# HGRN2 level products: one run and one PSUM bank per head half

## The chip, the cores and the metric

The kernel runs on one core of a Trainium2 chip. The metric is the device time of one execution in microseconds. Three runs of the kernel before took 2713.78, 2715.27 and 2718.02 us; the median is 2715.27 us. The profile comes from one further execution, which took 2714.48 us and whose span, from its first to its last instruction, is 2712.6 us.

## The reference

One layer of a hybrid decoder over 2048 prompt tokens and 32 sample tokens of width 1024: RMSNorm, an input projection whose columns feed four mixers (S5, HGRN2, RWKV-7, pooling), an output projection with a residual, RMSNorm, a squared-ReLU MLP with a residual, and a last RMSNorm. The change lies in the HGRN2 mixer, a gated linear recurrence:

```python
def step(S, inp):
    qb, kb, vb, gb = inp
    b = jnp.cumsum(gb, axis=2)
    diff = jnp.where(causal, b[:, :, :, None, :] - b[:, :, None, :, :], -jnp.inf)
    att = jnp.einsum('bhtk,bhsk,bhtsk->bhts', qb, kb, jnp.exp(diff))
    o = jnp.einsum('bhts,bhsv->bhtv', att, vb) + jnp.einsum('bhtk,bhkv->bhtv', qb * jnp.exp(b), S)
    ...
```

The kernel works on chunks of 64 tokens. `att` needs the decay between every two tokens of a chunk. It is built in levels: for a distance h of 32, 16, 8, 4, 2 and 1, the later half of each group of 2h tokens meets its earlier half, with both decays taken against the token in the middle. Every level is a matrix product of its own, of which a mask keeps the entries that belong to the level; the diagonal is a seventh product.

## The kernel before

The tokens go through in six blocks of 256 or 384 (`BLK`). Per block the main work is three dense stages, the input projection (`inproj`), the output projection (`outproj`) and the MLP (`mlp`). Their matmuls are at L157 to L159, three for each pair of 128x128 weights and tokens, since weights and activations are split into a high and a low part (L128 on ScalarE, L129 on VectorE). There are 13248 of them.

Beside the main work run the mixers of the next block as side work. `mixers` alternates between two lanes: `lane1` is RWKV-7, and `lane2` is pooling, then HGRN2 (`hgrn_pair`, once for each 128 tokens, so 16 times in all), then S5. Lanes are Python generators: each `yield` ends a step, and `drive` takes `RATIO` = 2 side steps for each step of the main work. In the first stage (blocks 0 and 1) `weave` and a `drive` with other ratios do the same. The steps set the order in which instructions are emitted; a scheduler of the framework then places them on the engines' queues by its own estimate of when each is ready. So the order on an engine is not simply that of the code, and it is fixed before the run.

In `hgrn_pair`, a pair is two chunks (`cp`) of 64 tokens, four heads as two tiles (`j`) of two halves (`hp`, 64 partitions each). Per pair the level part is this:

- 8 diagonal products (64x64 by 64x64) and 48 level products (64x64 by 64x32), all at L1272. They are float32, and the trace holds two records for each: 16 and 96 per pair.
- They go in two passes: first the diagonal and levels 0 and 1, then levels 2 to 5 (`for l0, l1 in ((-1, 2), (2, 6))`). Each pass takes two new PSUM buffers (`pas`, one for each head half) with 256 of their 512 columns in use. The lane has two such buffers in all (`PX`), so the second pass needs both back from the first.
- VectorE takes the results out after each pass: 2 multiplications with the diagonal mask (L1280) and 24 `copy_predicated` (L1287) per pair.
- Inside the first pass there is a `yield` after level 0 and inside the second one after level 3 (`YH`), then one after each pass's products and one after each pass's evacuation: six steps.

TensorE works with tiles: a 64x64 product uses a quarter of the array. In the profile the tile stands as 64\*64, 64\*128, 128\*64 or 128\*128 (rows and columns in use); the main matmuls are 128\*128.

Of the kernel before, what the change touches and what calls it, by code (L numbers as in the profile page):

```python
# [11 lines left out]
ALU = mybir.AluOpType  # L12
# [567 lines left out]
PX = (2, 2)  # L580
S0PM = True
PLATE = ()
YH, YS, YR = (0, 3), True, True


class Carve:
# [20 lines left out]
class Mix(Main):  # L607
# [580 lines left out]
    def hgrn_pair(self, b, c0, pool):  # L1188
        nc = self.nc
        tt, ts, stt = nc.vector.tensor_tensor, nc.vector.tensor_scalar, nc.vector.scalar_tensor_tensor  # L1190
        act, mm = nc.scalar.activation, nc.tensor.matmul
# [5 lines left out]
        q, f, v, gt = P[:, 2:4, W], P[:, 4:6, W], P[:, 6:8, W], P[:, 8:10, W]  # L1197
# [10 lines left out]
        k = T("E")  # L1208
# [9 lines left out]
        QK = T("QK", (128, 6, 256))  # L1218
# [19 lines left out]
        LV = (32, 16, 8, 4, 2, 1)  # L1238
        for li, h in enumerate(LV):
            nb = 256 // (2 * h)  # L1240
# [9 lines left out]
            O = QK[:, li, :].rearrange("p (j n s) -> p j n s", j=2, s=2 * h)[:, :, :, h:]  # L1250
            tt(out=O, in0=O, in1=q.rearrange("p j (n s) -> p j n s", s=2 * h)[:, :, :, h:], op=ALU.mult)

        for l0, l1 in ((-1, 2), (2, 6)):
            pas = [self.px() for _ in range(2)]
            sec = {}
            for l in range(l0, l1):
                o0 = 0 if l < 0 else 64 * (l - l0) + (64 if l0 < 0 else 0)
                w = 64 if l < 0 else 32
                for hp in range(2):
                    hs = slice(64 * hp, 64 * hp + 64)  # L1260
                    d = pas[hp][:, o0:o0 + 2 * w].rearrange("p (j n) -> p j n", j=2)
                    sec[l, hp] = d
                    for j in range(2):
                        for cp in range(2):
                            o = 128 * j + 64 * cp
                            if l < 0:
                                a, c = k[hs, j, 64 * cp:64 * cp + 64], q[hs, j, 64 * cp:64 * cp + 64]
                            else:
                                h = LV[l]
                                a = QK[hs, l, o:o + 64]  # L1270
                                c = a.rearrange("p (n s) -> p n s", s=2 * h)[:, :, h:]
                            mm(d[64 * cp:64 * cp + 64, j, :], a, c, start=True, stop=True)  # L1272
                if l in YH:
                    yield
            yield
            for l in range(l0, l1):
                for hp in range(2):
                    o, d = v[:, :, 64 * hp:64 * hp + 64], sec[l, hp]
                    if l < 0:
                        tt(out=o, in0=d, in1=self.C("i64")[:, None, :].to_broadcast([128, 2, 64]), op=ALU.mult)  # L1280
                        continue
                    h = LV[l]
                    nb = 32 // h
                    cut = lambda x: x.rearrange("p (n s) -> p n s", s=2 * h)[:, :, h:]
                    m = self.C("lv%d" % h).bitcast(mybir.dt.int32).rearrange("p (n s) -> p n s", s=h)
                    for j in range(2):
                        nc.vector.copy_predicated(cut(o[:, j, :]), m, d[:, j, :].rearrange("p (n s) -> p n s", s=h))  # L1287
            yield
        S = [self.S[:, (self.Si + i) % 3] for i in range(3)]
        self.Si = (self.Si + 2) % 3  # L1290
        pu = self.px()[:, :256].rearrange("p (c j n) -> p c j n", c=2, j=2)
# [8 lines left out]
        for j, cp, hp, o in jch:  # L1300
            w = slice(64 * cp, 64 * cp + 64)
            mm(po[o, j, w], VB[:, cp, 2 * j + hp, :], v[:, j, o], start=j == cp == 0, stop=False, skip_group_check=True)
        for j, cp, hp, o in jch:
            w = slice(64 * cp, 64 * cp + 64)
# [732 lines left out]
```

## Time and profile before

| | |
|---|---|
| median of three runs | 2715.27 us |
| the profiled execution | 2714.48 us |
| its span | 2712.6 us |
| TensorE busy (PE) | 2629.4 us, 97% |
| VectorE busy (DVE) | 1955.7 us, 72% |
| ScalarE busy (ACT) | 1438.6 us, 53% |
| mean granted TensorE clock | 0.982 of 2.4 GHz |

A matmul's record lasts longer than the array needs for it, since successive matmuls overlap; a row that says 0.34 us is followed by the next after about 0.175 us. So durations of TensorE's records are not added up here: what a stretch of matmuls takes is read from the start of one row to the start of a later one.

### The profile page before, as it was taken

The page shows a single profiled execution, that of the slowest core. Times are in us where ns is not written, and L with a number is a line of the kernel's source. Part 1 is how long each engine was busy: PE and PEld are TensorE (multiplying, and loading weights), DVE is VectorE, ACT ScalarE, POOL GpSimd, SP SyncE. Part 2 cuts the span into 40 slices and gives each one's busy share as a digit, 9 for nine tenths or more (in the row PEclk, how much of TensorE's full clock was granted, in tenths as well). Part 3 has the DMA queues.
Part 4 walks back from the last instruction along what each step waited for, and adds up shares of the span by engine and source line. Part 5 has one row for each costly group of instructions (what it writes and reads, how often), then busy time and mean ns, then how long its engine had stood idle before and what let it go on. Part 6 is the DMA issues. An engine that isn't in the chain of part 4 may idle for free.

```text
span 2712.6 us, 52883 instructions
## 1 busy us (share of the span) xinstructions
PE 2629.4 (97%) x20466; PEld 2492.0 (92%) x20466; DVE 1955.7 (72%) x4324; ACT 1438.6 (53%) x2377; POOL 357.5 (13%) x864
## 2 busy tenths in 40 slices
PE   8799899899999999999999999999999999999998
PEld 8688799889999999999999999999999989899997
DVE  7886888874877777487777748777775786557666
ACT  6544766544656545375654536565454754445443
POOL 7631201100111100001110010111001100000000
PEclk9799999999999999999999999999999999999999
DMA  6543344564333255532335553223555334435553
GB/s 208 142 126 98 124 148 134 156 190 147 115 96 98 96 166 165 166 119 88 99 101 174 167 160 113 94 91 107 173 177 159 100 103 122 133 115 169 167 168 127
DMA packets 221068, 366.28 MB, mean 135 GB/s; under 512 B 105520, under 2 KB 140912, under 8 KB 220816
## 3 DMA queue, kind: packets, MB, share of 16 engines
q1 hardware_dynamic: 220816, 362.90, 43.1%
q8 instruction: 161, 2.64, 0.4%
q14 instruction: 91, 0.75, 0.1%
HBM read 343.26 MB, written 17.99 MB: 133 GB/s over the span
## 4 chain that ended last, share of the span: by engine, by line
PE 74%; DVE 11%; DMA 5%; ACT 4%; POOL 3%; issue 2%; SPq 1%; DVEq 0%; ACTq 0%; POOLq 0%
PE mm L157 21%; PE mm L158 21%; PE mm L159 21%; DVE wlo L129 3%; DMA raw<-w 2%; PE x L1272 1%; ACT whi L128 1%; POOL XD L887 1%; POOL tm L885 1%; DMA xs<-xT 1%; PE x L687 1%; PE x L1828 1%; PE x L1827 1%; DMA mt<-dB 1%; PE x L951 1%
## 5 line engine op out<-in xcount | busy, mean ns | idle before, releaser
L128 ACT CAST whi<-raw 128x1024 fp32r<-128x1024 f32 x552 | 577.5, 1046 | 773.0 <-PE mm L158 528.0
L157 PE MATMUL mm<-AB,whi 128*128 128x384 f32 (+2 forms) x2880 | 950.4, 331 | 14.2 <-ACT whi L128 5.2
L159 PE MATMUL mm<-AB,wlo 128*128 128x384 f32 (+2 forms) x2880 | 936.2, 325 | 4.2 <-DVE wlo L129 3.8
L158 PE MATMUL mm<-AB,whi 128*128 128x384 f32 (+2 forms) x2880 | 935.2, 325 | 1.0 <-DVE AB L199 0.8
L129 DVE TENSOR_TENSOR wlo<-raw,whi 128x1024 fp32r<-128x1024 f32 x552 | 678.4, 1230 | 274.2 <-ACT whi L128 271.6
L157 PEld LDWEIGHTS mm<-AB,whi 128*128 128x128 f32 x2880 | 545.9, 190 | 27.3 <-ACT whi L128 6.3
L159 PEld LDWEIGHTS mm<-AB,wlo 128*128 128x128 f32 x2880 | 547.1, 190 | 9.3 <-DVE wlo L129 6.3
L158 PEld LDWEIGHTS mm<-AB,whi 128*128 128x128 f32 x2880 | 547.6, 190 | 6.7 <-DVE AB L199 1.4
L157 PE MATMUL mm<-act,whi 128*128 128x384 f32 (+2 forms) x1536 | 497.7, 329 | 4.6 <-ACT whi L128 2.5
L158 PE MATMUL mm<-act,whi 128*128 128x384 f32 (+2 forms) x1536 | 493.9, 323 | 0.5 <-DVE act L329 0.3
L159 PE MATMUL mm<-act,wlo 128*128 128x384 f32 (+2 forms) x1536 | 492.2, 322 | 0.0
L157 PEld LDWEIGHTS mm<-act,whi 128*128 128x128 f32 x1536 | 289.6, 190 | 12.9 <-DVE h L338 2.8
L158 PEld LDWEIGHTS mm<-act,whi 128*128 128x128 f32 x1536 | 291.2, 190 | 5.5 <-issue 2.3
L159 PEld LDWEIGHTS mm<-act,wlo 128*128 128x128 f32 x1536 | 290.6, 190 | 1.6 <-issue 0.2
L338 DVE TENSOR_TENSOR h<-h,mm 128x384 f32<-128x384 f32 (+2 forms) x384 | 192.5, 510 | 96.4 <-PE mm L159 95.6
L885 POOL TENSOR_TENSOR tm<-sq,XD 32x15 f32<-32x15 f32 (+7 forms) x240 | 90.7, 378 | 563.0 <-DMA sq<-XC 545.6
L329 DVE TENSOR_TENSOR act<-q,act 128x384 fp32r<-128x384 f32 (+2 forms) x192 | 98.9, 516 | 6.2 <-ACT q L326 1.7
L324 ACT ACTIVATE act<-r 128x384 fp32r<-128x384 f32 (+2 forms) x192 | 94.2, 490 | 13.3 <-DVE r L323 11.0
L887 POOL TENSOR_TENSOR XD<-XD,tm 32x15 f32<-32x15 f32 (+7 forms) x240 | 85.4, 356 | 18.5
L880 POOL MEMSET XD<- 32x512 f32 x16 | 8.3, 516 | 578.2 <-PE x L969 346.1
L192 DVE TENSOR_TENSOR acc<-acc,sq 128x384 f32<-128x384 f32 (+2 forms) x126 | 64.8, 514 | 15.7 <-ACT sq L191 13.3
L328 DVE TENSOR_TENSOR q<-r 128x384 f32<-128x384 f32 x128 | 71.1, 555 | 0.6 <-ACT r L321 0.5
(584 smaller groups left out, 3110.4 us busy)
## 6 DMA issues: line engine op xcount, KB each, us to landing
raw<-w SPq DMA_DIRECT2D x552, 512.0 KB
xs<-xT SPq DMA_DIRECT2D x96, 192.0 KB
yT<-xo SPq DMA_DIRECT2D x32, 192.0 KB
mt<-dB SPq DMA_DIRECT2D x20, 256.0 KB
mt<-dT SPq DMA_DIRECT2D x20, 256.0 KB
mt<-dC SPq DMA_DIRECT2D x20, 256.0 KB
xs<-xT SPq DMA_DIRECT2D x24, 144.0 KB
rt<-dRot SPq DMA_DIRECT2D x16, 98.0 KB
```

What stands on the lines that cost most here:

```text
L128: nc.scalar.copy(hi, raw)
L129: (nc.gpsimd if GW(i) else nc.vector).tensor_tensor(out=lo, in0=raw, in1=hi, op=ALU.subtract)
L157: nc.tensor.matmul(ps[:, :n], a, xh, start=k == ks[0], stop=False)
L158: nc.tensor.matmul(ps[:, :n], a, xl, start=False, stop=False)
L159: nc.tensor.matmul(ps[:, :n], c, xh, start=False, stop=k == ks[-1])
L192: nc.vector.tensor_tensor(out=acc[:, :n], in0=acc[:, :n], in1=q[:, :n], op=ALU.add)
L324: nc.scalar.activation(out=self.act[:, s, 0, :n], in_=r[:, :n], func=AF.Square)
L328: nc.vector.tensor_tensor(out=q[:, :n], in0=r[:, :n], in1=r[:, :n], op=ALU.mult)
L329: nc.vector.tensor_tensor(out=self.act[:, s, 1, :n], in0=q[:, :n], in1=self.act[:, s, 0, :n], op=ALU.subtract)
L338: nc.vector.tensor_tensor(out=self.h[:, d, :n], in0=self.h[:, d, :n], in1=ps[:, :n], op=ALU.add)
L885: g.tensor_tensor(out=w, in0=U[:, 0:t, t:t + 1].to_broadcast([32, t, m]), in1=XT[:, t:t + 1, t:16].to_broadcast([32, t, m]), op=ALU.mult)
L887: g.tensor_tensor(out=XT[:, 0:t, t:16], in0=XT[:, 0:t, t:16], in1=w, op=ALU.add)
```

## The change

The two passes become one. All seven products of a head half go to one PSUM buffer, the diagonal in columns 0 to 127 and level l in columns 128 + 64 l to 191 + 64 l: 512 columns, a full bank. The 56 products of a pair are emitted without a step between them. Then comes a `yield`, the evacuation of the diagonal and levels 0 and 1, a `yield`, the evacuation of levels 2 to 5, and a `yield`: three steps. Number, shape and operands of the products and of the evacuations stay, and so does their order in the code (`HO` puts the head half outermost, as the loops did).

```diff
-YH, YS, YR = (0, 3), True, True
+YS, YR = True, True
+HO = [(j, cp, hp) for hp in range(2) for j in range(2) for cp in range(2)]
...
-        for l0, l1 in ((-1, 2), (2, 6)):
-            pas = [self.px() for _ in range(2)]
-            sec = {}
-            for l in range(l0, l1):
-                o0 = 0 if l < 0 else 64 * (l - l0) + (64 if l0 < 0 else 0)
...
-                if l in YH:
-                    yield
-            yield
-            for l in range(l0, l1):
...
-            yield
+        pas = [self.px() for _ in range(2)]
+        sec = {}
+        for l in range(-1, 6):
+            w, o0 = (64, 0) if l < 0 else (32, 128 + 64 * l)
+            for hp in range(2):
+                sec[l, hp] = pas[hp][:, o0:o0 + 2 * w].rearrange("p (j n) -> p j n", j=2)
+            for j, cp, hp in HO:
...
+                mm(sec[l, hp][64 * cp:64 * cp + 64, j, :], a, c, start=True, stop=True)
+        yield
+        for l in range(-1, 6):
...
+            if l == 1:
+                yield
+        yield
```

In the changed kernel the products are at L1267 and the evacuations at L1273 and L1279. How the scheduler places them shows on TensorE in the second pair of block 3. Before, the pair's 56 products stand there in nine rows between the main matmuls (L157 to L159) and the products of the other lane (L687 sums over a head, L907, L908 and L913 transposes, L926 a 64x64 product); the first of them:

```order
L159 MATMUL mm<-AB_78,wlo 128x384
L1272 MATMUL x<-P_7462,E 64x64 x8
L1272 MATMUL x<-QK 64x32
L687 MATMUL x<-hi,bonesr 128x256
L687 MATMUL x<-lo,bonesr 128x256
L1272 MATMUL x<-QK 64x32 x2
L907 MATMUL x<-cst,Z 128x128
L908 MATMUL x<-cst,P_8323 128x128
L907 MATMUL x<-cst,Z 128x128
L908 MATMUL x<-cst,P_8323 128x128
L1272 MATMUL x<-QK 64x32 x5
L157 MATMUL mm<-act,whi 128x384
```

and most of the second pass of the same pair:

```order
L159 MATMUL mm<-act,wlo 128x384
L1272 MATMUL x<-QK 64x32 x4
L687 MATMUL x<-hi,bonesr 128x256
L799 MATMUL x<-tha,wl 128x128 x2
L687 MATMUL x<-lo,bonesr 128x256
L802 MATMUL x<-kx,wl 128x128 x2
L1272 MATMUL x<-QK 64x32 x12
L157 MATMUL mm<-act,whi 128x384
```

Of the changed kernel, the same pair (L988 is a product of the RWKV lane with 128\*64 tiles):

```order
L159 MATMUL mm<-AB_78,wlo 128x384
L1267 MATMUL x<-P_7569,E 64x64 x8
L1267 MATMUL x<-QK 64x32 x4
L988 MATMUL x<-sv,M_8879 64x64 x4
L1267 MATMUL x<-QK 64x32 x44
L157 MATMUL mm<-AB_78,whi 128x384
```

All 56 stand between two main matmuls now, with one piece of the other lane among them.

## Rows read from the trace of the kernel before

**Rows 1.** The page: the span, and busy time, share and instructions by engine.
```profile
span 2712.6 us, 52883 instructions
PE 2629.4 (97%) x20466; PEld 2492.0 (92%) x20466; DVE 1955.7 (72%) x4324; ACT 1438.6 (53%) x2377; POOL 357.5 (13%) x864
```

**Rows 2.** Windows: length, busy us by engine, granted clock, DMA share, GB/s.
```profile
85.00:135.00 50.00, 40.83 (x325) 35.85 (x324) 48.23 (x103) 28.57 (x51) 29.39 (x50) 0.80 0.58 155
...
0.00:135.00 135.00, 108.86 (x808) 100.03 (x809) 106.23 (x230) 77.13 (x133) 92.93 (x241) 0.86 0.59 176
135.00:365.00 230.00, 213.33 (x1943) 196.46 (x1942) 174.96 (x463) 128.82 (x229) 54.59 (x121) 0.95 0.41 122
365.00:640.00 275.00, 261.81 (x2462) 246.90 (x2463) 214.74 (x503) 157.71 (x263) 27.23 (x74) 0.98 0.49 152
640.00:1110.00 470.00, 468.78 (x3464) 446.14 (x3463) 337.81 (x734) 250.15 (x402) 47.68 (x115) 1.00 0.41 129
1110.00:1580.00 470.00, 469.50 (x3468) 446.78 (x3468) 337.37 (x734) 250.28 (x402) 48.00 (x115) 1.00 0.41 129
...
2050.00:2440.00 390.00, 381.64 (x2931) 355.17 (x2930) 267.06 (x639) 196.93 (x352) 38.43 (x81) 0.99 0.40 121
2440.00:2713.00 273.00, 256.19 (x1873) 254.32 (x1872) 179.57 (x286) 127.09 (x190) 0.00 (x0) 0.98 0.48 157
```

**Rows 3.** TensorE's longest waits: who for whom, us in total, times, longest.
```profile
PE x L1272 <- ACT E L1209: 8.5, 1, 8.5
PE mm L157 <- ACT whi L128: 7.7, 5, 2.8
```

**Rows 4.** Groups by shape, L1272: busy us, mean ns, idle before them.
```profile
L1272 PE MATMUL x<-QK 64*64 64x32 f32 x1536 | 52.1, 223 | 0.3 <-DVE P L1287 0.3
L1272 PE MATMUL x<-P,E 64*64 64x64 f32 x256 | 13.3, 232 | 11.1 <-ACT E L1209 8.5 <-ACT VB L1234 2.6
```

**Rows 5.** Timeline of TensorE from 755.6: start us, length us, instruction.
```profile
755.64 0.34 PE L158 MATMUL mm<-act,whi 128*128 128x384 f32 x1
755.82 0.33 PE L159 MATMUL mm<-act,wlo 128*128 128x384 f32 x1
756.08 0.45 PE L1272 MATMUL x<-QK 64*64 64x32 f32 x16
756.46 0.44 PE L157 MATMUL mm<-AB,whi 128*128 128x384 f32 x1
```

**Rows 6.** The same from 765.9.
```profile
765.89 0.34 PE L159 MATMUL mm<-AB,wlo 128*128 128x384 f32 x1
766.16 0.69 PE L1272 MATMUL x<-QK 64*64 64x32 f32 x32
766.78 0.45 PE L157 MATMUL mm<-AB,whi 128*128 128x384 f32 x1
```

**Rows 7.** The same from 875.3.
```profile
875.34 0.34 PE L159 MATMUL mm<-act,wlo 128*128 128x384 f32 x1
875.61 0.68 PE L957 MATMUL x<-XD,M 64*64 64x64 f32 x16
876.22 0.45 PE L157 MATMUL mm<-act,whi 128*128 128x384 f32 x1
```

**Rows 8.** The same from 920.1.
```profile
920.13 0.34 PE L159 MATMUL mm<-act,wlo 128*128 128x384 f32 x1
920.39 0.47 PE L926 MATMUL x<-Z 64*64 64x64 f32 x16
920.68 0.67 PE L1272 MATMUL x<-QK 64*64 64x32 f32 x32
921.27 0.44 PE L157 MATMUL mm<-act,whi 128*128 128x384 f32 x1
```

**Rows 9.** Line L1287: its instructions' ns (min/median/max), who waited for it.
```profile
L1287 DVE COPY_PREDICATED P<-cst,x x384: 165/188/227, 106.3 to 2257.5; 128x32 f32<-128x32 int32 x192
...
PEld x L951: 0.8, 3
PE x L1272: 0.3, 1
```

More of the change, by code (lines that the diff above doesn't have):

```diff
@@ L1251, in hgrn_pair @@
             tt(out=O, in0=O, in1=q.rearrange("p j (n s) -> p j n s", s=2 * h)[:, :, :, h:], op=ALU.mult)
-        for l0, l1 in ((-1, 2), (2, 6)):
-            pas = [self.px() for _ in range(2)]
-            sec = {}
-            for l in range(l0, l1):
-                o0 = 0 if l < 0 else 64 * (l - l0) + (64 if l0 < 0 else 0)
[L1258 to L1272, printed above, removed]
-                if l in YH:
-                    yield
-            yield
-            for l in range(l0, l1):
[L1277 to L1287, printed above, removed]
-            yield
@@ new lines, in hgrn_pair @@
+        pas = [self.px() for _ in range(2)]
[5 more added lines that the diff above has]
+            for j, cp, hp in HO:
+                hs, o = slice(64 * hp, 64 * hp + 64), 128 * j + 64 * cp
+                if l < 0:
+                    a, c = k[hs, j, 64 * cp:64 * cp + 64], q[hs, j, 64 * cp:64 * cp + 64]
+                else:
+                    a = QK[hs, l, o:o + 64]
+                    c = a.rearrange("p (n s) -> p n s", s=2 * LV[l])[:, :, LV[l]:]
+                mm(sec[l, hp][64 * cp:64 * cp + 64, j, :], a, c, start=True, stop=True)
@@ new lines, in hgrn_pair @@
+        yield
+        for l in range(-1, 6):
+            for hp in range(2):
+                o, d = v[:, :, 64 * hp:64 * hp + 64], sec[l, hp]
+                if l < 0:
+                    tt(out=o, in0=d, in1=self.C("i64")[:, None, :].to_broadcast([128, 2, 64]), op=ALU.mult)
+                    continue
+                h = LV[l]
+                cut = lambda x: x.rearrange("p (n s) -> p n s", s=2 * h)[:, :, h:]
+                m = self.C("lv%d" % h).bitcast(mybir.dt.int32).rearrange("p (n s) -> p n s", s=h)
+                for j in range(2):
+                    nc.vector.copy_predicated(cut(o[:, j, :]), m, d[:, j, :].rearrange("p (n s) -> p n s", s=h))
+            if l == 1:
+                yield
```

## The prediction

> **What bounds the kernel now.** I read the page's share of busy time first, then the windows by stage, then TensorE's waits, and last the timeline around single runs of level products.
>
> TensorE is busy for 97% of the span, VectorE for 72%, ScalarE for 53% [rows 1]. The windows say where the other 3% lie [rows 2]. From 640 to 1580 us TensorE is busy for 468.78 and 469.50 of two times 470 us at a granted clock of 1.00 (the stretch from 1580 to 2050 reads the same): nothing else can set the time there, and whatever leaves TensorE's queue shortens the kernel by as much. From 2050 to 2440 it is 381.64 of 390. Before 640 us it is different: 26 us of the first 135 pass without a matmul, then 17 of 230 and 13 of 275, and the clock reads 0.86, 0.95 and 0.98. The clock has two levels, 1.2 and 2.4 GHz, so a mean of 0.86 over 135 us is 2 x 0.14 x 135 = 38 us at the lower one. By the same working the next two stretches spend 23 and 11 us there. The longest wait of all is one of 8.5 us, early, of the first pair's diagonal product for ScalarE; the next in sum are 7.7 us for a split weight [rows 3].
>
> So the question is what the change does to TensorE's queue: first in the bound part (from 640 us on), then in the first stage, where it also matters who waits.
>
> **The change part by part.** No product and no evacuation is added or removed. The level products' records cost 52.1 and 13.3 us of busy time as they stand [rows 4], and the same records remain. What changes is with whom they stand together, and that has a price.
>
> Price of a run. Between two main matmuls lies 0.18 us from start to start [rows 5]. With 16 level records between them it is 756.46 - 755.82 = 0.64 us, 0.46 more [rows 5]; with 32 records it is 766.78 - 765.89 = 0.89 us, 0.71 more [rows 6]. So 16 more records cost 0.25 us, 0.0155 us each, and 0.46 - 0.25 = 0.21 us of a run does not depend on its length. That is the price of leaving the 128x128 tile for 64x64 and coming back: two switches, 0.105 us each. I call this the low price.
>
> A second view gives a higher one. Sixteen 64x64 records alone take 876.22 - 875.34 - 0.18 = 0.70 us more than no side work [rows 7], and 32 level records alone 0.71 [rows 6]. Where two such runs stand together they take 921.27 - 920.13 - 0.18 = 0.96 us [rows 8], not 1.41. One join (two switches fewer) is worth 0.45 us here, 0.225 per switch; the two kinds also run into each other in the array. I call this the high price.
>
> How many switches go. I counted over TensorE's whole order of both kernels where the tile shape of one matmul differs from that of the one before. It is 781 times before and 732 times in the changed kernel, 49 fewer. Runs of level products with nothing else between them go from 126 to 62. The loss is not even: up to the 2880th of the 13248 main matmuls (about 620 us) the count rises from 226 to 240, since the scheduler cuts the other lanes' work there into more pieces; behind it, where TensorE sets the time, it falls from 554 to 491, by 63: in the three middle blocks from 140, 140 and 142 to 118 each, and in the last it rises from 132 to 137. The pieces shown above are an example: eight runs of a pair become two.
>
> The sum. Bound part: 63 switches at 0.105 to 0.225 us are 6.6 to 14.2 us less. First stage: 14 more at the same prices are 1.5 to 3.2 us more, and nothing where TensorE would have waited anyway. Together 49 switches, -5.1 to -11.0 us. I take 0.15 us, nearer to the low price: most of the joins are of level products with level products, as between rows 5 and rows 6, and not with the other lane's products. That is 49 x 0.15 = 7.4 us less.
>
> The missing steps. A pair has three steps fewer, so the HGRN lane is nine steps shorter in a block of three pairs, and the rest of the side work stands earlier among the main matmuls. In the bound part this is worth nothing by itself: the same work is done by the same busy engine, and its side work already ends well before the block does. What hides it is the main work behind, which waits for no mixer until the next block; if that cover were gone, a late mixer would show as a wait of the output projection, and the largest sums of waits are others [rows 3].
>
> The second pass's wait. Before, the second pass needed both PSUM buffers back from VectorE. TensorE stood idle for it for 0.3 us in the whole span [rows 9]. Taking the wait away is worth 0 to 0.3 us.
>
> The later evacuation. In the code VectorE begins only behind all 56 products, not behind the first 24; the run in between is 64 records x 0.0155 = 1.0 us. Then 24 copies of 0.188 us, 4.5 us, follow as before [rows 9]. Queued behind them on VectorE are weight splits (L129), for which main matmuls wait in the end. With VectorE busy for 338 of 470 us [rows 2] a delay of 1.0 us is caught up within a few microseconds; without that cover it is 16 x 1.0 = 16 us at most. I take 0.
>
> The first stage by itself. In the changed order the first pair's level products end three projection tiles earlier there and the second pair's seven, and the pieces of S5 and RWKV around them move, on SyncE's queue too (some loads of S5's matrices swap places with weights). There are 56 us without a matmul and 72 us at the lower clock in it. A different order can give or take some of that; nothing in the rows says which way. I take 0, with 6 us either way as an estimate (a tenth of the idle time).
>
> Against the profiled execution's own time: 2714.48 - 7.4 = 2707.1 us. That execution is 0.8 us below the median of the runs, so for the median the forecast is 2715.27 - 7.4 = 2707.9 us.
>
> **The rivals.**
>
> *Faster by less than can be told.* The switch is cheap (the low price), the first stage's 14 new switches all cost, and the reordered first stage gives a few microseconds back: 49 x 0.105 = 5.1 us less in TensorE's queue, and with up to 5 us lost early the time is 2710 to 2715 us. For it: rows 5 and 6, which are the cleanest. Against it: rows 8, and that in the bound part alone 63 x 0.105 = 6.6 us go.
>
> *Slower: the first stage loses clock.* In the changed order the side work of the first stage stands closer together in places: between the 960th and the 1440th main matmul there are 171 side products for 114 before. In this trace a stretch dense with small products and waits shows the lower clock: from 85 to 135 us it reads 0.80, which is 2 x 0.20 x 50 = 20 us at 1.2 GHz and costs 10 us [rows 2]. If two such stretches come in addition, that is 20 us more, and the time is 2707.9 + 20 = 2728 us; it is slower than before from about 13 us on. Against it: in the bound part, with just as many side products in places, the clock reads 1.00 throughout. The Trainium skill (TensorE: Matmul & The Clock Gate, section on the HAM clock gate) says that the lower clock is the default and that activity releases it. By that rule fewer waits between the products would bring the clock up and not down, so that dense runs help; the trace agrees from 640 us on, and cannot tell for the first stage, where waits and small products come together.
>
> *The level run does not do what it says.* The scheduler could still cut the runs; it does so in the first stage, and two to seven pieces stay for a pair in the middle blocks. That is in the count already.
>
> *More than forecast.* The high price holds, and the first stage finds the HGRN results earlier and waits less: 11 us and up to 6 more, 2698 us.
>
> **How the numbers follow.** About 0.2%, 5.4 us, is what a measurement of this kernel can tell from no change, so the forecast counts as faster below 2709.8 us. The forecast with prices from 0.12 us up, together with the last rival, has a chance of 0.60 (of which 0.12 is the last rival). Too small a gain, or one that the first stage gives back, has 0.29. Slower by over 5.4 us, above all by the clock, has 0.11. The range of 8 in 10 goes from 2697 us (the high price and 6 us of the first stage) to 2717 us (the low price and some 7 us lost early): below it I leave one in 20, above it some three in 20. The likeliest case's own range is 2702 to 2710 us.
>
> **What would show it.** In the profile after: the level products of the bound part in runs of 48 and more records, and from main matmul to main matmul around 48 records about 0.95 us more than the bare 0.18, by the low price. The three middle blocks, 470 us each now, lose some 22 switches each and come out at 465 to 468 us, with TensorE as busy as before. TensorE's waits from 640 us on stay near nothing. The prediction is wrong if the middle blocks keep their 470 us (the switch had cost nothing), if waits for L129 appear in them (the later evacuation), or if the first stage, up to the end of the fifth pair, moves by more than the whole of the rest.

## The result and the profile after

The changed kernel is slower. Its median is 2739.1 us of four runs (2732.8 to 2740.7), against 2714.53 us for the kernel before (four runs, 2713.6 to 2718.02): a ratio of 1.0072, 95% interval 1.0057 to 1.0086. The forecast was 2707.9 us, 2697 to 2717. The profiled execution took 2737.62 us. Its page begins like this, in answer to [rows 1]:

```profile
span 2735.8 us, 52850 instructions
PE 2634.5 (96%) x20466; PEld 2501.6 (91%) x20466; DVE 1956.2 (72%) x4324; ACT 1437.2 (53%) x2377; POOL 351.7 (13%) x864
```

The span is 23.2 us longer and TensorE is busy for only 5.1 us more, with the same 20466 matmul records. So most of the loss is time without a matmul. To see where, I cut both traces at the same places, behind the 2880th, 5280th, 7440th, 9600th and 11520th of the 13248 main matmuls (the first stage, the three middle blocks, the last block with side work, the rest). Windows of the kernel after, cut there (length; busy us of PE, PEld, DVE, ACT and POOL; granted clock, DMA share, GB/s):

```profile
0.00:632.00 632.00, 574.12 (x5118) 532.68 (x5119) 490.23 (x1189) 357.28 (x617) 178.69 (x435) 0.93 0.47 145
632.00:1138.00 506.00, 500.54 (x3658) 479.37 (x3657) 350.87 (x751) 261.26 (x419) 44.75 (x115) 1.00 0.41 131
1138.00:1603.00 465.00, 458.63 (x3419) 437.26 (x3418) 333.50 (x729) 246.83 (x399) 46.20 (x115) 1.00 0.40 127
1603.00:2056.00 453.00, 447.69 (x3416) 427.10 (x3415) 329.88 (x729) 244.56 (x401) 44.70 (x115) 0.99 0.41 128
2056.00:2486.00 430.00, 419.30 (x3127) 393.13 (x3126) 286.38 (x666) 210.94 (x372) 37.38 (x84) 0.98 0.40 119
```

The kernel before, cut at the same places:

```profile
0.00:622.00 622.00, 566.00 (x5113) 526.06 (x5113) 488.14 (x1185) 355.61 (x613) 174.75 (x435) 0.94 0.49 148
622.00:1128.00 506.00, 504.78 (x3665) 481.48 (x3664) 354.35 (x754) 264.44 (x423) 47.68 (x115) 1.00 0.41 129
1128.00:1589.00 461.00, 460.50 (x3417) 437.78 (x3416) 332.81 (x729) 247.27 (x399) 48.00 (x115) 1.00 0.41 129
1589.00:2039.00 450.00, 449.27 (x3414) 426.19 (x3414) 329.11 (x728) 243.28 (x399) 47.26 (x115) 1.00 0.41 129
2039.00:2464.00 425.00, 416.64 (x3130) 390.17 (x3130) 287.19 (x667) 211.47 (x375) 39.79 (x84) 0.99 0.41 122
```

Read the second number against the first. In the second middle block TensorE's busy time falls from 460.50 to 458.63, as the joined runs should make it, but the block grows from 461 to 465 us: 6.4 us are idle, where before 0.5 were. In the other two middle blocks the idle time also rises, from 1.2 to 5.5 us and from 0.7 to 5.3. The first stage loses 10 us and some clock, the last block 5 us. TensorE's longest waits of the kernel after (for whom, us in total, times, longest), beside [rows 3]:

```profile
PE x L1267 <- ACT E L1210: 13.6, 2, 8.5
PE mm L157 <- ACT whi L128: 9.1, 7, 2.7
PE x L688 <- ACT lw L808: 7.3, 3, 2.4
...
PE mm L159 <- DVE wlo L129: 5.3, 8, 0.9
```

The third row is new, and it is regular: three waits of 2.4 us, one in each middle block, right behind main matmuls 3997, 6205 and 8413, that is 2208 apart. L688 is a sum over a head; here it is the one of the RWKV lane's preparation. L808 is an activation of the same lane on ScalarE, which reads the PSUM buffer that this sum needs next. The first wait on TensorE's timeline (start us, length us, instruction, idle time before it):

```profile
866.38 0.39 PE L688 MATMUL x<-hi,bonesr 128*128 128x256 f32 x1 [2.42 <-ACT lw L808]
866.60 0.41 PE L158 MATMUL mm<-AB,whi 128*128 128x384 f32 x1
...
867.34 0.52 PE L157 MATMUL mm<-AB,whi 128*128 128x384 f32 x1
867.66 0.52 PE L158 MATMUL mm<-AB,whi 128*128 128x384 f32 x1
...
870.36 0.33 PE L158 MATMUL mm<-AB,whi 128*128 128x384 f32 x1
870.53 0.34 PE L159 MATMUL mm<-AB,wlo 128*128 128x384 f32 x1
```

The wait is paid twice here. The queue stays in order: main matmul L158 at 866.60 does not pass the waiting sum. And behind the wait the main matmuls start 0.32 us apart, before it and from 870.19 on 0.175. Windows before, in and behind this stretch:

```profile
860.00:863.90 3.90, 3.90 (x23) 3.60 (x22) 2.60 (x8) 3.84 (x6) 0.00 (x0) 1.00 0.00 0
863.90:866.40 2.50, 0.08 (x2) 0.03 (x1) 2.50 (x8) 2.49 (x8) 0.00 (x0) 1.00 0.17 36
866.90:870.10 3.20, 3.20 (x12) 3.20 (x11) 3.20 (x11) 2.88 (x6) 0.00 (x0) 0.50 0.24 97
870.10:874.00 3.90, 3.90 (x25) 3.86 (x24) 3.90 (x10) 3.83 (x7) 0.00 (x0) 1.00 0.37 137
```

The granted clock reads 0.50 right behind the wait: 1.2 GHz. In the kernel before, at the same product (its line is L687 there), TensorE passes without a pause, and in its profile the clock never falls between 622 and 2039 us:

```profile
852.34 0.34 PE L159 MATMUL mm<-AB,wlo 128*128 128x384 f32 x1
852.51 0.28 PE L687 MATMUL x<-hi,bonesr 128*128 128x256 f32 x1
```

What ScalarE did while TensorE waited, in the kernel after:

```profile
857.80 1.28 ACT L1204 ACT_TABLE_LOAD   x1
859.10 0.42 ACT L1204 ACTIVATE E<-E 128x256 f32<-128x256 f32 x1
...
859.84 1.28 ACT L1205 ACT_TABLE_LOAD   x1
...
863.26 1.28 ACT L1210 ACT_TABLE_LOAD   x1
864.56 0.42 ACT L1210 ACTIVATE E<-L 128x256 f32<-128x256 f32 x1
864.88 0.35 ACT L805 COPY P<-x 128x256 f32<-128x256 f32 x1
865.13 0.37 ACT L808 ACTIVATE lw<-x,dv 128x128 f32<-128x128 f32 x1
```

L1204, L1205 and L1210 are the gates of the block's third HGRN pair, with a table load each. Before, the RWKV lane's L807 ran at 850.47 with none of them ahead of it. The third pair's L1203 (L1204 in the kernel after) came only at 878.9. With three steps fewer for each pair, the third pair has moved in front of this piece of RWKV.

So there are two theories. *A, the placement*: the missing steps move the lanes against each other, the fixed order on TensorE then asks for operands that are not ready, and each wait also costs clock. *B, the run or the bank*: the joined run or the full bank itself costs time, by switches that are dearer or cheaper than read, or by buffers held longer.

### The profile page after: what moved, and what is told of

Read it like the earlier page. It is cut to its first block, busy times and chain, and to the rows that moved or that the text cites. A ratio compares the mean times of both kernels' runs of the same rounds, so it can differ in the third digit from the quotient of the medians.

```text
span 2735.8 us, 52850 instructions
## 1 busy us (share of the span) xinstructions
PE 2634.5 (96%) x20466; PEld 2501.6 (91%) x20466; DVE 1956.2 (72%) x4324; ACT 1437.2 (53%) x2377; POOL 351.7 (13%) x864
## 4 chain that ended last, share of the span: by engine, by line
PE 66%; DVE 12%; DMA 7%; ACT 5%; POOL 4%; issue 3%; SPq 3%; DVEq 0%; ACTq 0%; POOLq 0%
PE mm L157 19%; PE mm L159 19%; PE mm L158 18%; DVE wlo L129 3%; DMA raw<-w 2%; POOL XD L888 2%; POOL tm L886 1%; ACT whi L128 1%; DMA xs<-xT 1%; DMA mt<-dT 1%; SPq L892 1%; PE x L688 1%; PE x L1267 1%; SPq L1828 1%; DVE xn L216 1%
## 5 line engine op out<-in xcount | busy, mean ns | idle before, releaser
L157 PE MATMUL mm<-AB,whi 128*128 128x384 f32 (+2 forms) x2880 | 954.5, 332 | 10.8 <-ACT whi L128 6.4
L159 PE MATMUL mm<-AB,wlo 128*128 128x384 f32 (+2 forms) x2880 | 942.7, 328 | 5.3 <-DVE wlo L129 5.3
L158 PE MATMUL mm<-AB,whi 128*128 128x384 f32 (+2 forms) x2880 | 941.4, 327 | 0.6 <-DVE AB L1186 0.3
L129 DVE TENSOR_TENSOR wlo<-raw,whi 128x1024 fp32r<-128x1024 f32 x552 | 679.1, 1231 | 313.7 <-ACT whi L128 310.9
L157 PEld LDWEIGHTS mm<-AB,whi 128*128 128x128 f32 x2880 | 552.8, 192 | 21.9 <-ACT whi L128 7.7
L159 PEld LDWEIGHTS mm<-AB,wlo 128*128 128x128 f32 x2880 | 553.1, 192 | 12.3 <-DVE wlo L129 7.2
L158 PEld LDWEIGHTS mm<-AB,whi 128*128 128x128 f32 x2880 | 553.2, 192 | 5.8 <-DVE AB L1186 0.7
L157 PE MATMUL mm<-act,whi 128*128 128x384 f32 (+2 forms) x1536 | 495.6, 329 | 5.4 <-DVE h L338 2.8
L158 PE MATMUL mm<-act,whi 128*128 128x384 f32 (+2 forms) x1536 | 493.0, 322 | 0.0
L159 PE MATMUL mm<-act,wlo 128*128 128x384 f32 (+2 forms) x1536 | 491.8, 323 | 0.0
L157 PEld LDWEIGHTS mm<-act,whi 128*128 128x128 f32 x1536 | 288.6, 189 | 12.5 <-DVE h L338 3.9
L158 PEld LDWEIGHTS mm<-act,whi 128*128 128x128 f32 x1536 | 290.6, 189 | 4.3 <-issue 2.1
L159 PEld LDWEIGHTS mm<-act,wlo 128*128 128x128 f32 x1536 | 289.4, 189 | 2.3 <-issue 1.0
L886 POOL TENSOR_TENSOR tm<-sq,XD 32x15 f32<-32x15 f32 (+7 forms) x240 | 82.9, 345 | 571.9 <-DMA sq<-XC 554.5
L324 ACT ACTIVATE act<-r 128x384 fp32r<-128x384 f32 (+2 forms) x192 | 94.3, 491 | 16.2 <-DVE r L323 13.6
```

The source lines that it names most:

```text
L129: (nc.gpsimd if GW(i) else nc.vector).tensor_tensor(out=lo, in0=raw, in1=hi, op=ALU.subtract)
L157: nc.tensor.matmul(ps[:, :n], a, xh, start=k == ks[0], stop=False)
L158: nc.tensor.matmul(ps[:, :n], a, xl, start=False, stop=False)
L159: nc.tensor.matmul(ps[:, :n], c, xh, start=False, stop=k == ks[-1])
L324: nc.scalar.activation(out=self.act[:, s, 0, :n], in_=r[:, :n], func=AF.Square)
L886: g.tensor_tensor(out=w, in0=U[:, 0:t, t:t + 1].to_broadcast([32, t, m]), in1=XT[:, t:t + 1, t:16].to_broadcast([32, t, m]), op=ALU.mult)
```

## The experiments

The stages in us, cut at the places named above (the start of the next main matmul in each trace), with the changes of tile shape over TensorE's whole trace (780 and 731 there, where the prediction counted 781 and 732). Ratios are to the kernel before on the same chip, with 95% intervals; its medians there were 2714.53 to 2720.22 us. The stage columns come from one profile each and are not corrected for the chip. How far one order can spread: four profiles with the order of before (before, bank alone and, up to the last block, the two kernels of the price of a switch) read 621.8 to 626.4 us in the first stage and 1417.3 to 1419.7 over the middle blocks, and the first two of them 424.9 and 429.4 in the last. Differences of that size tell nothing.

| kernel | first stage | middle blocks | last block | changes | median us | ratio |
|---|---|---|---|---|---|---|
| before | 621.9 | 505.7, 461.1, 450.5 | 424.9 | 780 | 2714.53 | 1 |
| after | 631.7 | 506.1, 464.8, 453.4 | 430.6 | 731 | 2739.1 | 1.0072 [1.0057, 1.0086] |
| six steps | 615.0 | 509.5, 463.6, 457.1 | 433.1 | 721 | 2730.79 | 1.005 [1.0033, 1.0067] |
| five steps | 629.7 | 515.1, 467.3, 458.2 | 426.9 | 689 | 2748.12 | 1.0112 [1.0091, 1.0134] |
| two passes, three steps | 643.6 | 509.7, 465.8, 457.0 | 427.6 | 734 | 2749.62 | 1.0119 [1.0098, 1.0141] |
| bank alone | 626.4 | 506.7, 461.3, 450.4 | 429.4 | 780 | 2718.39 | 0.9998 [0.9986, 1.0009] |
| steps at the end | 636.8 | 502.1, 460.2, 452.1 | 427.0 | 732 | 2731.17 | 1.0042 [1.0026, 1.0057] |
| third pair held | 632.3 | 506.9, 461.9, 451.2 | 431.3 | 709 | 2734.14 | 1.0069 [1.0051, 1.0087] |
| other buffer | 645.5 | 511.8, 469.5, 457.1 | 441.3 | 670 | 2775.22 | 1.0207 [1.018, 1.0233] |
| no table loads | 633.0 | 504.6, 466.4, 452.1 | 426.7 | 731 | 2733.82 | 1.0068 [1.0052, 1.0084] |
| mixed steps | 618.2 | 503.1, 458.6, 448.0 | 422.3 | 707 | 2696.57 | 0.9928 [0.9914, 0.9942] |
| two passes, mixed steps | 621.1 | 506.0, 458.5, 447.4 | 430.4 | 722 | 2712.64 | 0.9982 [0.9971, 0.9992] |
| the same with the bank | 623.6 | 505.9, 457.8, 447.9 | 426.5 | 722 | 2709.22 | 0.9971 [0.9957, 0.9985] |

**The steps and the bank, apart.** Six steps again, as empty ones, around the one run and the full bank:

```diff
         yield
+        yield
         for l in range(-1, 6):
...
             if l == 1:
                 yield
+                yield
+                yield
```

> The changed kernel with its one run of 56 products and its full bank, but six steps per pair again: one empty step more behind the products and two more between the two evacuations. Theory A (three missing steps bring the third pair's first ScalarE work of the HGRN lane onto that of the RWKV lane, TensorE waits about 2.4 us there in each middle block, and a stretch at 1.2 GHz follows): the wait of L688 for L808 and the stretch of 1.2 GHz in the middle blocks are gone; with 721 changes of tile shape for 780 it is 59 x 0.1 to 0.2 = 6 to 12 us faster than before, 2702 to 2709 us. Theory B (the long run and the full bank themselves cost the time): it stays at 2733 to 2741 us.

Theory A's time, 2702 to 2709 us, did not come: at 2730.79 us it is still slower than before, and lies just below theory B's range. Against the changed kernel it is 1.005 for 1.0072, and the intervals overlap. What it gains is all in the first stage (615.0 for 631.7), and there it is mostly clock: the two traces have the same idle time in that stage, 57.8 and 57.9 us, but 47.8 and 88.7 us at 1.2 GHz. The 2.4 us waits for L808 are gone; other waits have come, for a load and for ScalarE:

```profile
PE x L1781 <- DMA rt<-dRot: 9.5, 3, 3.3
...
PE x L688 <- ACT hi L685: 5.7, 5, 2.4
```

So the number of steps alone does not give the old placement back. The same with one empty step less at the last place, five in all:

> The changed kernel with five steps per pair (one empty step more behind the products, one more between the evacuations). Theory A: the time follows from where the lanes meet, not from the number of steps in a straight line; with 689 changes of tile shape it is 2705 to 2735 us, and its waits from 640 us on say which. Theory B: 2733 to 2741 us as the changed kernel.

It has 42 changes fewer than the changed kernel and is slower than it (1.0112 for 1.0072), and slower than either theory's range (2748.12 us). The count of switches does not order the kernels.

The kernel before with two passes and half banks, but only three steps:

```diff
-YH, YS, YR = (0, 3), True, True
+YH, YS, YR = (), True, True
...
-            yield
+            if l0 > 0:
+                yield
```

> The kernel before with its two passes and half-filled banks, but three steps per pair as in the changed kernel (no step inside a pass, none between the first evacuation and the second pass). Theory A: as slow as the changed kernel, 2730 to 2745 us, with the waits of about 2.4 us once in each middle block. Theory B: as the kernel before or faster, 2704 to 2716 us (734 changes of tile shape for 780).

Here neither run nor bank is changed, and it is slower than the changed kernel and than theory A's range (2749.62 us; the first stage alone takes 643.6). Its waits include the same one, behind the same main matmuls (3997, 6205, 8413):

```profile
PE x L687 <- ACT lw L807: 7.2, 3, 2.4
PE x L1272 <- DVE P L1287: 6.3, 4, 2.9
```

The first row is the wait of the changed kernel; the second is the second pass that waits for its buffers, 0.3 us in [rows 9] and 6.3 us now. The kernel before with only the bank changed, every engine's order untouched:

```diff
+        pas = [self.px() for _ in range(2)]
         for l0, l1 in ((-1, 2), (2, 6)):
-            pas = [self.px() for _ in range(2)]
...
-                o0 = 0 if l < 0 else 64 * (l - l0) + (64 if l0 < 0 else 0)
+                o0 = 0 if l < 0 else 128 + 64 * l
```

> The kernel before with only the bank of the change: both passes write to one pair of PSUM buffers, the diagonal and levels 0 and 1 in columns 0 to 255, levels 2 to 5 in 256 to 511; passes, steps and the order on every engine are those of before, instruction for instruction. Theory A (the order and the meeting of the lanes cost the time, the bank does not): 2713 to 2716 us, within 0.2% of before. Theory B (the full bank costs the time): 2725 us or more.

No change. Theory B's bank falls, and steps without the run are enough for the loss.

**The price of a switch.** Two kernels with the same 256 extra small products (64x64 by 64x32) in the last block's MLP, where no side work runs. In the first they stand in one run of 8 in each of 32 tiles of the MLP, in the second in four runs of 2 (cut; the comments give the second kernel's values):

```diff
+                if k in (3,):             # second kernel: (1, 3, 5, 6)
+                    for i in range(8):    # second kernel: range(2)
+                        z = 64 * (i % 2)
+                        nc.tensor.matmul(pz[z:z + 64, 32 * (i // 2):32 * (i // 2) + 32], self.C("i64")[0:64, :], self.C("tril")[0:64, 0:32], start=True, stop=True)
```

> The kernel before with something added to the last block's MLP, where no side work is: eight dummy 64x32 products (64x64 tiles) for each of the 32 up tiles, in one run behind the fourth pair of parts; they add work, the outputs stay. By the price of a run (0.21 us and 16 x 0.0155 us) 32 runs add 32 x 0.46 = 15 us: about 2730 us.

> The same 256 dummy products in the same place, but in four runs of two for each up tile: 998 changes of tile shape over the order for 848. By the low price, 0.105 us each, 16 us more than with one run; by the high price, 0.225 us, 34 us more; if a change of tile shape costs nothing, the same time.

They took 2743.12 us (ratio 1.0085 [1.007, 1.01]) and 2768.15 us (1.0177 [1.0162, 1.0193]). The orders have 848 and 998 changes of tile shape, and 25.0 us / 150 = 0.167 us each. It lies between the low and the high price of the prediction; 0.15 was taken. The one run missed its own forecast: 22.9 us more than before on that chip (2720.22), for 15. A run of the changed kernel gives a similar price:

```profile
880.37 0.34 PE L158 MATMUL mm<-AB,whi 128*128 128x384 f32 x1
880.81 0.92 PE L1267 MATMUL x<-QK 64*64 64x32 f32 x48
881.66 0.44 PE L159 MATMUL mm<-AB,wlo 128*128 128x384 f32 x1
```

From 880.37 to 881.66 are 1.29 us, 1.11 more than the bare 0.18 (0.95 were forecast). Less 48 x 0.0155 that leaves 0.37 for two switches, 0.18 each. Not every run agrees: three such runs in the kernel with the other buffer (below) take 0.94 us, as forecast. Either way the joins are worth about what the prediction said, and the loss is elsewhere.

**Where the lanes stand.** One run and bank, with the three steps given back behind the pair instead of inside the level part:

```diff
         yield from self.hgrn_out(b, W, po, 256, T)
+        yield
+        yield
+        yield
```

> The changed kernel with its three missing steps put back as empty ones at the end of the pair, behind its output part, so that only the next pair is held back. Theory A: the third pair's first ScalarE work meets the RWKV lane's no more at the place where L688 waits 2.4 us; with 732 changes of tile shape 2715 to 2732 us, and the waits from 640 us on say how much the rest of the new order costs. Theory C (any order but the one of before runs into some wait of each middle block, whatever the steps): 2728 to 2750 us, with other waits of 1 to 4 us in each middle block.

The middle blocks come down to 1414.4 us in sum, from 1424.3 after and 1417.3 before, and the waits for L808 are gone; the first stage gets worse (636.8). The six-step kernel was the other way round. The time, 2731.17 us, lies in the ranges of both theories that were named for it and decides between neither. Three steps before the third pair only, in blocks 2 to 4:

```diff
+                if b > 1 and c == 256:
+                    yield
+                    yield
+                    yield
                 yield from self.hgrn_pair(b, c, pool)
```

> The changed kernel with three empty steps in front of the third HGRN pair in blocks 2, 3 and 4 only. Theory A: the three waits of 2.4 us of L688 for L808 are gone; up to the 2880th main matmul it is as the changed kernel. With 709 changes of tile shape for 731, 5 to 15 us less than the changed kernel, if no other wait comes. Theory C (any other order has its own waits): other waits of 1 to 4 us come in their place and the gain stays under 5 us.

This missed. It was to move the third pair back and take the wait for L808 away. The wait stayed, 3 x 2.4 us, one main matmul from the old place:

```profile
PE x L688 <- ACT lw L808: 7.2, 3, 2.4
```

So a step more in the lane's code is not a step later for each of its instructions. The RWKV head sum in a PSUM buffer of the main work, so that it does not stand in line for the lane's:

```diff
-        pss = self.px(1)
+        pss = self.psum()
```

> The changed kernel, but the sum over a head in the RWKV preparation (the L688 that waits) takes a PSUM buffer of the main matmuls and not one of the two that L808 has to read first. Theory A: the wait of 2.4 us and the 1.2 GHz stretch behind it (some 1.6 us) go in each of three middle blocks, 12 us, and with 670 changes of tile shape for 731 some 6 to 10 us more: 2717 to 2722 us; less of it if the main matmuls then wait for a buffer. Theory B: 2733 to 2741 us.

This missed by most: 1.0207, the slowest of all with the fewest changes of all (670). The sums, which now share the main work's buffers, wait longer, and so do the main matmuls:

```profile
PE mm L688 <- ACT hi L685: 15.5, 7, 5.6
PE mm L157 <- ACT whi L128: 12.4, 5, 3.7
```

**Are the table loads the cause of the wait?** The third pair's Exp, Ln and Exp become Abs in blocks 2 to 4, which leaves these functions out and needs no new table: the trace has 165 loads for 171. The order on TensorE, VectorE, GpSimd and SyncE stays as it is:

```diff
-        act(out=E, in_=E, func=AF.Exp, scale=-1.0)
-        act(out=L, in_=E, func=AF.Ln, bias=1.0)
+        low = b > 1 and c0 == 256
+        act(out=E, in_=E, func=AF.Abs if low else AF.Exp, scale=-1.0)
+        act(out=L, in_=E, func=AF.Abs if low else AF.Ln, bias=1.0)
...
-        act(out=k, in_=L, func=AF.Exp, scale=-1.0)
+        act(out=k, in_=L, func=AF.Abs if low else AF.Exp, scale=-1.0)
```

> The changed kernel, but in the third HGRN pair of blocks 2, 3 and 4 the first Exp, Ln and Exp on ScalarE become Abs, which needs no function table of its own: the three preparations leave those functions out, so the HGRN results of these pairs are not the reference's. The order on TensorE, VectorE, GpSimd and SyncE is that of the changed kernel, instruction for instruction; ScalarE has 6 table loads of 1.28 us fewer in the whole program, two for each of the three pairs. Theory A (L688 waits because the HGRN lane's table loads stand before L808 on ScalarE): the wait of 2.4 us and the 3.4 us at 1.2 GHz behind it are gone in each of three middle blocks, some 4 us each, and the time is 8 to 12 us below that of the changed kernel. If the wait has another cause: the same time as the changed kernel, and the same three waits.

The wait went and the time stayed. TensorE's timeline of this kernel, at the head sum and then 7.7 us later at the third pair's diagonal products:

```profile
865.32 0.38 PE L688 MATMUL x<-hi,bonesr 128*128 128x256 f32 x1
...
873.02 0.40 PE L1268 MATMUL x<-P,E 64*64 64x64 f32 x7
875.45 0.27 PE L1268 MATMUL x<-P,E 64*64 64x64 f32 x2 [2.03 <-ACT VB L1236]
```

And of the changed kernel at the same products:

```profile
875.32 0.35 PE L1267 MATMUL x<-P,E 64*64 64x64 f32 x10
875.49 0.19 PE L1267 MATMUL x<-QK 64*64 64x32 f32 x1
```

Without the loads TensorE passes the head sum at once and comes to the pair 2 us early; there it waits 2.0 us for the copy to VB by which ScalarE empties the PSUM buffer of the pair's transposes; the run needs one of the lane's two buffers. Either way the level products begin in earnest at about 875.4 us (this trace reached the block 1.3 us later, at 633.0 us for 631.7, so it is 1.2 us sooner counted from there). All three middle blocks do this: waits for VB of 6.1 us in sum have come for 7.3 us of waits for L808, and the idle time there is 17.5 us for 17.2. TensorE, which takes its queue in order, meets the third pair some 2 us before ScalarE is done with it, and pays at the one place or the other. That no table load matters is not shown: ahead of the copies to VB stands a load of the RWKV lane (L822, 1.28 us from 872.79). What is shown is that the six loads, two ahead of each wait for L808, are not by themselves the loss.

**A placement that waits for nothing much.** The six-step kernel had the best first stage, the steps at the end the better middle blocks. Both together, by block:

```diff
         yield
+        for _ in range(3 if b < 2 else 0):
+            yield
         S = [self.S[:, (self.Si + i) % 3] for i in range(3)]
...
         yield from self.hgrn_out(b, W, po, 256, T)
+        for _ in range(3 if b > 1 else 0):
+            yield
```

> A version that takes the best stage of each: one run and a full bank, in blocks 0 and 1 with three empty steps behind the evacuation (six steps, as in the run with six steps, whose first stage was 7 us shorter than that of before), from block 2 on with three empty steps at the end of the pair (whose middle blocks took 1414 us for 1417 of before). If the stages add up: 7 us less than before, ratio 0.997. If the order of one stage depends on the one ahead: between 0.997 and 1.005.

2696.57 us, ratio 0.9928: faster than the kernel before and the changed one, and faster than forecast (0.997). Up to the 2880th main matmul TensorE's order is that of the six-step kernel, record for record. Its windows, cut at the same places:

```profile
0.00:618.00 618.00, 559.67 (x5111) 518.60 (x5112) 485.14 (x1182) 351.83 (x608) 174.93 (x435) 0.96 0.48 147
618.00:1121.00 503.00, 500.74 (x3662) 478.63 (x3661) 354.80 (x756) 264.41 (x424) 43.94 (x115) 1.00 0.42 132
1121.00:1580.00 459.00, 456.94 (x3420) 436.15 (x3419) 332.89 (x728) 246.31 (x399) 43.70 (x115) 1.00 0.41 129
1580.00:2028.00 448.00, 445.59 (x3418) 424.23 (x3417) 329.57 (x728) 242.06 (x398) 44.40 (x115) 1.00 0.41 129
```

About 2 us are idle in each middle block, for 5 to 6 in the changed kernel, and the clock stays. The three blocks take 7.6 us less than before; their changes fall from 422 to 368, and 54 x 0.167 = 9.0 us; 4.3 us more idle time take part of that back. So most of the forecast gain is there, in the blocks for which it was forecast. Two passes with the same steps, first with half banks and then with the full one, show how much of it is the one run (the edit of the first, against the kernel before):

```diff
-                if l in YH:
+                if l in YH and b < 2:
                     yield
...
-            yield
+            if l0 > 0 or b < 2:
+                yield
...
+        for _ in range(3 if b > 1 else 0):
+            yield
```

> The steps of the hybrid without the change's one run and bank: two passes with half-filled banks, in blocks 0 and 1 the six steps of the kernel before, from block 2 on three in the level part and three empty ones at the end of the pair. If the hybrid's gain comes from the steps alone: as the hybrid, ratio to before 0.990 to 0.996. If one run and one bank earn it: 0.998 to 1.008, with TensorE waiting for L1287 between the passes (6.3 us in the run with two passes and three steps).

> As the run before it, with its order on every engine instruction for instruction, but with the full bank, so that the second pass needs no buffer back. If the bank is worth what TensorE waits for L1287 without it, and 1.2 GHz behind such waits: 3 to 10 us less than the run before it, and no wait for L1287. If not: the same time.

Placed in this way, two passes are 0.2 to 0.3% faster than before, the one run 0.7%. In the middle blocks the three are equal within 3 us, and so are their changes (364 and 368): fewer steps inside the passes let the scheduler join the products nearly as well as the one run does. The one run's lead lies in the first stage (618.2 us for 621.1 and 623.6) and the last block (422.3 for 430.4 and 426.5); the latter two have one and the same order, so part of that lead is spread. The two banks' intervals overlap: nothing can be told from them. The changed kernel once more, beside the mixed steps:

> The changed kernel once more, on the chip of these runs. All theories: slower than before by 0.5 to 0.9%, with the waits of L688 for L808 at the same place of each middle block.

2735.14 us, ratio 1.0067 [1.0052, 1.0082], with the same three waits (2.4 to 2.8 us). Its first stage takes 630.1 us.

## Why the prediction was wrong

**The step that failed** is the one on the missing steps: "In the bound part this is worth nothing by itself: the same work is done by the same busy engine, and its side work already ends well before the block does." The work is indeed the same. But the steps fix the order, the order decides whether TensorE finds its operands, and a busy engine has no slack in which to make up a wait. The only cover that I looked at was the mixer's end, which the main work does not meet until the next block. I did not ask whether each small product, at its new place, would still come after its operand from ScalarE. That two passes with three steps lose more than the change does, without run or bank, and that the same run and bank range from 0.9928 to 1.0112 with only empty steps moved, shows it. By stage, against 0.15 us for each change: the middle blocks are 17 us off (+7.0 for -10.2), the first stage 8 (+9.8 for +2.1), the last block 5 (+5.7 for +0.8, and two later profiles of the same order read 429.6 and 426.7 us, so its share is not clear).

In the second middle block the terms are: waits +5.9 us, 3.4 us at 1.2 GHz +1.7 (half of them, at half the clock), and 22 changes fewer x 0.167 = -3.7. The sum is +3.9; measured is +3.7. Over all three it closes less well: idle time +14.7, of which the waits for L808 are 7.3; 13.6 us at 1.2 GHz +6.8; 68 changes fewer -11.4. The sum is +10.2; measured is +7.0. The same account fits every other order of the table: take the added idle time and half the added time at 1.2 GHz off a kernel's difference to before in the middle blocks, and 0.18 to 0.25 us are left as gain for each change that went (12 profiles), and 0.2 us or less in all where the order is that of before (3 profiles). So the count of changes alone does not order the kernels, but in the middle blocks the three terms together do. Why the gain is somewhat above 0.167 us here stays open.

**The price of a switch** was near, 0.167 us measured for 0.15 taken, but partly by luck, since both prices behind it were misread. The low one stops at the start of the first main matmul behind a run, and the next one then starts 0.28 us later and not 0.175. Behind a run of 32 records at 847.58 in the kernel before:

```profile
848.20 0.44 PE L157 MATMUL mm<-AB,whi 128*128 128x384 f32 x1
848.48 0.33 PE L158 MATMUL mm<-AB,whi 128*128 128x384 f32 x1
```

All 87 such places between 640 and 2040 us read 0.28 or 0.29. With these 0.105 us the low price is (0.21 + 0.105) / 2 = 0.16 us for each switch. The high one took the 0.70 us of L957's 16 records [rows 7] for the 16 of L926 [rows 8]. Those alone take less, as the changed kernel shows (L927 there):

```profile
841.06 0.34 PE L159 MATMUL mm<-act,wlo 128*128 128x384 f32 x1
841.33 0.47 PE L927 MATMUL x<-Z 64*64 64x64 f32 x16
841.73 0.45 PE L157 MATMUL mm<-act,whi 128*128 128x384 f32 x1
```

That is 841.73 - 841.06 - 0.18 = 0.49 us. The join of rows 8 is then worth 0.49 + 0.71 - 0.96 = 0.24 us, and with the 0.105 us 0.17 for each switch.

**The first stage** was put at 0, with 6 us either way. It lost 9.8. Its terms by the same sizes are 14 changes more, +2.3; waits +1.9; 13.6 us more at 1.2 GHz, +6.8 (half of it). By these the rival of the lost clock acted, at a third of its size. But the profile of the bank alone, which has the order of before, also shows 88.7 us at 1.2 GHz there and 626.4 us, so the clock's share can't be put down to the change. The loss itself can: the changed kernel's order in this stage reads 631.7, 630.1 and 633.0 us in three profiles (with the run without table loads), that of before 621.8 to 626.4 in four. The range of 6 us was too narrow: over the kernels here the stage takes 615 to 645 us.

**The rule of the Trainium skill** (TensorE: Matmul & The Clock Gate, section on the HAM clock gate), that activity releases the clock, agrees with the middle blocks of the changed kernel: the low stretches stand behind waits (866.7 us behind the wait that ended at 866.4), not in dense runs. What I missed is that the change would make waits.

**The second pass's wait** was right at 0 to 0.3 us, but only as the kernel before was placed; in the two-pass kernel with three steps it is 6.3. **The later evacuation** was right at 0: waits for L129 are 5.3 us for 3.8, with none in the middle blocks (0.5 us before), no matmul waits for L1279, and TensorE's weight loads wait 1.2 us for it in the whole span.

**The signs named in advance**: the long runs came (48 records in 1.11 us, for 0.95), and TensorE's busy time in the three middle blocks fell by 7.7 us. The middle blocks came out at 506, 465 and 453 us in these cuts, against 506, 461 and 450: not shorter, which had been named as a sign that a switch costs nothing. It costs something; the waits, which were to stay near nothing, hid it. The first stage moved more than the whole forecast, which was named as what would make it wrong.

**What stays open**: the scheduler's estimate against the chip was not read, so why one placement waits and the next does not is followed up only for the third pair, which TensorE meets 2 us too early. Why the first stage swings by 30 us from order to order is not settled. No placement here had less idle time in the middle blocks than before's, so the kernel before may owe its time to its order as much as to its passes; the runs do not tell these apart.

## What to carry to other kernels

Where one in-order engine is busy for nearly all of a stretch, an edit that moves steps must be costed by the place of each small product against its operands, and not by busy time alone. If a change that should save time makes a kernel slower, compare its waits at the same main matmul and then move empty steps about, block by block, before the change itself is blamed. When a wait goes away and the time stays, look for it a few microseconds further down the same queue.

## What the runs showed that I had not expected

A single wait of about 2 us in an otherwise busy stretch can be followed by 3.4 us at 1.2 GHz, which adds 1.7 us to it. From 640 to 2300 us of the changed kernel's profile there are seven such stretches, all behind a wait of 1.7 us or more, and none in the profile of the kernel before. It does not follow each time: a wait of 2.6 us at 2088.6 in the kernel before cost no clock, though in the bank alone, with the same order, waits of 2.2 and 2.4 us there did. In the second profile of the changed kernel the same three waits were there, but no low stretch in the first middle block, and one stretch (2174.3) stands behind a wait of only 1.1 us.

And kernels with the same products, shapes and operands lie between 0.9928 and 1.0119 of the kernel before by their order (and at 1.0207 with one PSUM buffer taken elsewhere), while the count of tile-shape changes, 0.167 us each, does not order them.
